# A fused convolution and attention block: the attention's output weight is placed in freed token quarters, later tokens' quarters are split one product later, and the merge takes late tokens first

## The chip, the cores and the metric

The kernel runs on one core of one Trainium2 chip. The metric is the device time of one execution in microseconds (us). The engines are named as the profile names them: PE (TensorE, matrix products), PEld (its weight loads), DVE (VectorE), ACT (ScalarE), POOL (GpSimd) and SP (SyncE, which issues nearly all transfers; its queue is in order, as are those of the others).

## The reference, cut to what matters

One decoder block on x of shape (1, 2048, 1024) in float32. All of its steps, with the names that the kernel uses:

```python
h = rms_norm(x, norm_w) * (1 + scale) + shift            # hT in the kernel
a, b, g_conv, q, k, v, g_attn, m_conv, m_attn = split(h @ w_in)
u = depthwise_causal_conv(a * sigmoid(b), conv_w, conv_b)    # 31 taps
u = silu(layer_norm(u)) * silu(g_conv)
y_conv = u @ w_conv_out                                  # yc
o = dilated_window_attention(rope(rms_norm(q)), rope(rms_norm(k)), v)  # 3 groups x 4 heads
o = sum over groups of softmax(lse) * o                  # the merge
y_attn = (o * silu(g_attn)) @ w_attn_out                 # ya; w_attn_out is 512 x 1024
y = sigmoid(m_conv) * y_conv + sigmoid(m_attn) * y_attn
out = x + gate * (y @ w_out)
```

## The kernel before, in words

Every matrix product is made in three passes: each float32 operand is split into a high part (ACT copies it to the type fp32r) and a low part (DVE or POOL subtracts the high part from the raw value), and high x high, high x low and low x high are added in PSUM. So each operand takes a transfer into a staging tile, a copy on ACT and a subtraction on DVE or POOL before PE can use it.

The kernel goes through these stages:

1. Start: norm and transposition of x into `hT`, high and low, in 16 tiles of 8 KB per partition: `h{hi,lo}{kh}{t}`, with kh the half of the 1024 channels and t the 512-token quarter. They fill the right end of the on-chip memory.
2. Twelve attention units (project, attend) over 16 token blocks each.
3. The merge: 32 steps, each for half the heads (`half` 0 or 1) and one block j of 128 tokens. A step computes the attention's gate (24 matmuls, tile `pzg`, function `z_tokens`, line 367), weighs the three groups (`om`, DVE and ACT), multiplies on POOL (`sg`, L512), transposes on PE (`pta`, L517) and writes `ai_d` to DRAM. The order is all blocks of half 0, then, for half 1, blocks 8 to 15, 4 to 7, 0 to 3. In the last 8 steps the sums S1 to S4 of token quarters (computed earlier, in DRAM as `s_d`) are put over quarters that are no longer read, four pieces of 256 columns each step (`quarter_place`: transfer L831, ACT copy L832, subtraction L833).
4. Two halves of 1024 tokens, each with 20 jobs. A job (`quad`) computes two 128-column blocks of a, b or a gate for 1024 tokens with seven products instead of eight (Strassen-Winograd: the token quarters are A11, A12, A22, S1 to S4; the weight quarters B11 to B22, T1 to T4). A product is 12 matmuls of 512 columns. PSUM copies by ACT (`kept`, L955) and sums on DVE and POOL stand between the products. After product n, `after(n)` prepares product n's weights of the next job (`column_steps`: POOL combines, L913; ACT copies, L918; subtraction L919), and runs some steps of the depthwise convolution on DVE (lines 995 to 1038), which is queued in `conv_todo` when its `ab_quad` is done. In the last job of the first half, `after(n)` instead replaces the quarter just used by the one of the later tokens: four pieces of 512 columns through seven landing tiles (`landing`).
5. Output: `ya` (32 blocks of 12 matmuls, `project`, L1171), layer norm of u beside it, `yc` (32 blocks of 24 matmuls), then the last product with w_out. Before this stage `start_output` closes the convolution's pool `cv`, opens the staging pool `fr` and the weight pool `wap` over its place, and loads and splits `w_attn_out` into `wah`, `wal` (L1098 to L1100). The split high and low parts of `ai_d` are `ai_0` to `ai_3`.

Where tiles of two pools share memory, the later tile waits for the last use of the earlier one. The order on PE is the order in the program (`manual_schedule`); on the other engines a scheduler orders the instructions ahead of time by the times that it expects.

Of the kernel before, what the change touches and what calls it, by code (L numbers as in the profile page):

```python
# [10 lines left out]
F32 = mybir.dt.float32  # L11
# [14 lines left out]
NH = 4  # L26
# [28 lines left out]
def tile_hybrid_block(  # L55
# [61 lines left out]
    with pool("start", side="right") as st:  # L117
# [564 lines left out]

    def quarter_load(half, k, names):
# [14 lines left out]
    for i in range(8):  # L698
        half, k = divmod(i, 4)
        at = NB * 4 + 1 + 12 * i  # L700
        for n, f in ((0, lambda half=half, k=k: quarter_load(half, k, (("21", 0, 0, 1), ("22", 1, 1, 1), ("11", 2, 0, 0)))),
                     (2, lambda half=half, k=k: quarter_sum(half, k, 1, "22", "21", "22", ALU.add)),
                     (4, lambda half=half, k=k: quarter_sum(half, k, 3, "21", "11", "21", ALU.subtract)),
                     (6, lambda half=half, k=k: quarter_sum(half, k, 2, "11", "22", "11", ALU.subtract)),
                     (7, lambda half=half, k=k: quarter_load(half, k, (("12", 1, 1, 0),))),
                     (10, lambda half=half, k=k: quarter_sum(half, k, 4, "12", "12", "11", ALU.subtract))):
            at_step((at + n) // NB, (at + n) % NB, 23, f)
# [118 lines left out]

    def quarter_place(half, name, k, cols, raw, eng):
# [3 lines left out]
        nc.sync.dma_start(raw, quarter_src(half, name, k)[:, cols])  # L831
        nc.scalar.activation(h, raw, AF.Copy)  # L832
        eng.tensor_tensor(l, raw, h.bitcast(F32), op=ALU.subtract)  # L833

    placing = [(n, k, c) for n in ("S2", "S3", "S4", "S1") for k in range(4) for c in (0, 256)]
    for half in range(2):
        for at_j, j in enumerate(orders[half]):
            if half == 0 and j < 3:
                continue
            if half == 1 and at_j >= 8:  # L840
                for i, (n, k, c0) in enumerate(placing[4 * (at_j - 8) : 4 * (at_j - 8) + 4]):
                    raw = wp.tile([P, 384], F32, tag="raw", name=f"raw{n}_{k}_{c0}", bufs=3)[:, :256]
                    quarter_place(0, n, k, slice(c0, c0 + 256), raw, nc.gpsimd if i % 2 else nc.vector)
            hooks = spread_load(loads[j - 4]) if half == 0 and 4 <= j < 4 + KC else {}
            while len(turns) >= 2:
                hooks.setdefault(3, []).append(turns.pop(0))
            pz = merge_z(half, j, cur, hooks)
            if j % 2 == 0:
                state["w"] = weighed.pop((half, j))
                following = pairs[pairs.index((half, j)) + 1 :][:1]  # L850
                coming = [load_pair(*p) for p in following]
            turns += merge_step(half, j, pz, state)
            if j % 2:
                for p, at in zip(following, coming):
                    weighed[p] = merge_weights(*p, at, wk, 2)
            if j == 3 and half == 0:
                queued.__exit__(None, None, None)
                nxt, loads = unit_weights(NG * NH + 1)
        cur = nxt
    for f in turns:  # L860
# [41 lines left out]
    def column_steps(c0, c1):  # L902
# [81 lines left out]
    def conv_parts(half, cb, ut):  # L984
# [16 lines left out]
        def odd(j):  # L1001
            def f():
# [4 lines left out]
                else:  # L1007
                    psum_o = box["o"]
                    if j == HT - 1:
                        box["o"] = cv.tile([P, 512], F32, tag="co", name=f"co{half}_{cb}")  # L1010
                    stt(box["o"], o[:, 2 + j : 514 + j], w, psum_o, op0=ALU.mult, op1=ALU.add)  # L1011
# [78 lines left out]

    big = {}

    def split(h, l, src, eng=nc.vector, raw=None):

# [18 lines left out]

    def big_pairs(tag, n):
        return [[big["wap"].tile([P, D], F32R, tag=f"wb{hl}{k}", name=f"{tag}{hl}{k}") for k in range(n)] for hl in "hl"]

    got, steps = job_columns(0)
    for f in steps:
        f()
    for i, (kind, half, g, cb) in enumerate(jobs):  # L1120
        last_of_half = i + 1 < len(jobs) and jobs[i + 1][1] > half
        nxt, steps = job_columns(i + 1) if i + 1 < len(jobs) else ([], [])
        if i + 1 == len(jobs):
            run_conv(len(conv_todo))
            wraw_c.__exit__(None, None, None)
            start_output()
# [15 lines left out]
        got = nxt  # L1142
    pe_order.__exit__(None, None, None)


    wpool_c.__exit__(None, None, None)
    hpool.__exit__(None, None, None)

# [100 lines left out]
    def load_ai(t, k):  # L1249
        ais[t, k] = parts(t // 2, f"ai{t}_{k}")  # L1250
        raw = gp.tile([P, 512], F32, tag="gt", name="airaw") if t == 0 and k == 3 else None
        split(*ais[t, k], ai_d[k, :, 512 * t : 512 * t + 512], raw=raw)

    wc = [[None] * KC, [None] * KC]

    def load_wc(half, k, h, l):
        split(h, l, w_conv_out[P * k : P * k + P, 512 * half : 512 * half + 512])
        wc[half][k] = h, l
# [42 lines left out]
    def split_wo(half, k):  # L1301
        h, l = (last["wo"][half].tile([P, 512], F32R, name=f"wo{half}{hl}{k}", bufs=1) for hl in "hl")
        split(h, l, w_out[P * k : P * k + P, 512 * half : 512 * half + 512])
        last[half, k] = h, l
# [54 lines left out]
    ys_c.__exit__(None, None, None)  # L1359
    big["pool"].__exit__(None, None, None)  # L1360
    wop_c.__exit__(None, None, None)
    wcp_c.__exit__(None, None, None)


# [26 lines left out]
```

## Time and profile before

| | us |
|---|---|
| median of 3 runs | 2499.51 (2499.28 to 2500.17) |
| the profiled execution's own time | 2502.48 |
| its span, first to last instruction | 2500.7 |
| PE busy | 2400.5 (96%) |
| DVE busy | 1747.3 (70%) |
| ACT busy | 971.0 (39%) |
| POOL busy | 799.2 (32%) |

Busy time is the time in which an engine worked on at least one instruction. A wait row names the instruction that stood still, what released it, the total, the number of waits and the longest. Window rows give the busy time of each engine with the number of its instructions, the clock granted to TensorE (1.00 is full), the share of the 16 DMA engines' time and the rate. The mean granted clock over the span is 0.981.

### The profile page before, as it was taken

To read this page: it belongs to the slowest core of one execution; us is meant where nothing else is said; L and a number is where in the kernel's file an instruction comes from. 1 tells how busy PE (TensorE), PEld (TensorE's weight loads), DVE (VectorE), ACT (ScalarE), POOL (GpSimd) and SP (SyncE) were. 2 spreads that over 40 slices of the span, in tenths; PEclk is the share of its full clock that TensorE was granted. 3 is DMA by queue.
4 is the path that set the end of the run, shared out by engine and by line. 5 is a ranking of instruction groups with operands and counts; after the bars stand their busy time and mean duration, and the time that the engine had idled before them with its cause. 6 is when DMAs were issued, how large, how long until landed. Compare 5 with 4: busy or idle time off the path is not lost.

```text
span 2500.7 us, 39106 instructions
## 1 busy us (share of the span) xinstructions
PE 2400.5 (96%) x12881; PEld 2140.7 (86%) x12881; DVE 1747.3 (70%) x3945; ACT 971.0 (39%) x2738; POOL 799.2 (32%) x925
## 2 busy tenths in 40 slices
PE   6999999999999999999899999799999949999999
PEld 2989999999999999999788888588888828888887
DVE  5855655555556555567699999999999956774333
ACT  4733343344334434445543444544444333331000
POOL 4421111111111111113766766866676400000000
PEclk8999999999999999999999999899999969999999
DMA  7633543454442221136432332623233287867343
GB/s 252 214 114 113 159 125 103 142 153 147 145 129 81 68 64 48 38 106 196 126 97 93 102 102 93 202 85 109 93 95 108 75 275 250 274 201 235 118 145 104
DMA packets 329736, 336.25 MB, mean 134 GB/s; under 512 B 27512, under 2 KB 251032, under 8 KB 329534
## 3 DMA queue, kind: packets, MB, share of 16 engines
q1 hardware_dynamic: 327758, 331.07, 42.3%
q10 hardware_dynamic: 1776, 2.69, 0.3%
q8 instruction: 103, 1.69, 0.3%
q14 instruction: 99, 0.81, 0.1%
HBM read 216.01 MB, written 117.64 MB: 133 GB/s over the span
## 4 chain that ended last, share of the span: by engine, by line
PE 81%; DVE 8%; DMA 5%; ACT 2%; issue 2%; POOL 1%; SPq 0%; DVEq 0%; ACTq 0%; POOLq 0%
PE pz L367 29%; PE out L1171 7%; PE yc L1171 7%; PE paab L949 6%; PE ya L1171 4%; PE pag_g_d L949 3%; PE pcab L949 3%; PE pag_mc_d L949 3%; PE ps L439 3%; PE po L458 3%; PE pag_ma_d L949 2%; PE ptq L429 2%; PE pcg_g_d L949 2%; PE pcg_mc_d L949 1%; PE pbab L949 1%
## 5 line engine op out<-in xcount | busy, mean ns | idle before, releaser
L367 PE MATMUL pz<-wh_u,hT_lo 128*128 128x384 f32 x1536 | 537.1, 350 | 4.9 <-DVE hT_lo L286 2.9
L367 PE MATMUL pz<-wh_u,hT_hi 128*128 128x384 f32 x1536 | 518.3, 337 | 5.6 <-ACT wh_u L343 2.8
L367 PE MATMUL pz<-wl_u,hT_hi 128*128 128x384 f32 x1536 | 519.0, 338 | 0.6 <-DVE wl_u L346 0.6
L395 DVE SCALAR_TENSOR_TENSOR qk<-pz,st,wqk 128x128 f32<-128x128 f32 x384 | 117.0, 346 | 317.9 <-POOL st L111 317.7
L110 POOL TENSOR_SCALAR st<-st 128x2 f32<-128x2 f32 x192 | 48.1, 251 | 812.6 <-ACT sq L384 812.6
L367 PEld LDWEIGHTS pz<-wh_u,hT_hi 128*128 128x128 f32 x1536 | 290.7, 189 | 8.4 <-ACT wh_u L343 3.5
L367 PEld LDWEIGHTS pz<-wh_u,hT_lo 128*128 128x128 f32 x1536 | 289.4, 188 | 8.1 <-DVE hT_lo L286 3.7
L367 PEld LDWEIGHTS pz<-wl_u,hT_hi 128*128 128x128 f32 x1536 | 289.8, 189 | 1.9 <-DVE wl_u L346 1.4
L431 ACT ACTIVATE qkT<-ptq 128x256 f32<-128x256 f32 x192 | 73.9, 385 | 420.3 <-PE ptq L429 419.8
L1027 DVE SCALAR_TENSOR_TENSOR ce<-us,pair_taps,ce 128x512 f32<-128x512 f32 x240 | 179.3, 747 | 2.3
L998 DVE SCALAR_TENSOR_TENSOR ce<-ut,chan,ce 128x512 f32<-128x512 f32 x240 | 178.4, 743 | 0.0
L1011 DVE SCALAR_TENSOR_TENSOR cq<-ut,chan,cq 128x512 f32<-128x512 f32 x208 | 155.7, 748 | 2.7
L384 ACT ACTIVATE sq<-pz 128x128 bf16<-128x128 f32 x384 | 106.2, 276 | 99.1 <-PE pz L367 92.2
L111 POOL TENSOR_TENSOR st<-st,mhalf 128x2 f32<-128x2 f32 x192 | 136.7, 712 | 16.0
L919 POOL TENSOR_TENSOR slT<-wB,shT 128x512 fp32r<-128x512 f32 x80 | 112.1, 1402 | 62.9 <-ACT shT L918 62.6
L913 POOL TENSOR_TENSOR wB<-wB,wB 128x512 f32<-128x512 f32 x80 | 107.7, 1346 | 72.4 <-DVE slB L919 66.6
L918 ACT ACTIVATE shB<-wB 128x512 fp32r<-128x512 f32 x120 | 75.3, 628 | 120.2 <-issue 93.3
L444 ACT ACTIVATE sm<-sm,osb 128x128 f32<-128x128 f32 (+1 forms) x192 | 88.7, 462 | 62.3 <-DVE osb L442 59.7
L1354 DVE TENSOR_TENSOR ot<-out,gate_row 128x512 f32<-128x512 f32 x32 | 22.1, 692 | 116.2 <-PE out L1171 116.2
L458 PE MATMUL po<-lv,pT 128*128 128x128 f32 x600 | 97.2, 273 | 0.0
L918 ACT ACTIVATE shT<-wB 128x512 fp32r<-128x512 f32 x120 | 74.7, 623 | 56.7 <-PE pcab L949 18.3
L458 PEld LDWEIGHTS po<-lv,pT 128*128 128x128 f32 x600 | 93.1, 189 | 0.5 <-issue 0.5
(614 smaller groups left out, 6401.5 us busy)
## 6 DMA issues: line engine op xcount, KB each, us to landing
wB<-in_w_in_dram SPq DMA_DIRECT2D x160, 256.0 KB, 3.4
qkv_d<-qkv SPq DMA_DIRECT2D x128, 192.0 KB, 2.2
raw_u<-in_w_in_dram SPq DMA_DIRECT2D x93, 192.0 KB, 2.9
lqk<-qkv_d SPq DMA_DIRECT2D x128, 128.0 KB, 2.4
acc_d<-osb SPq DMA_DIRECT2D x192, 65.0 KB, 1.7
at<-acc_d SPq DMA_DIRECT2D x64, 195.0 KB, 3.6
wada<-in_w_ada_dram SPq DMA_DIRECT2D x16, 512.0 KB, 8.5
lv<-qkv_d SPq DMA_DIRECT2D x128, 64.0 KB, 1.8
```

The costliest lines, as they stand in the source:

```text
L111: nc.gpsimd.tensor_tensor(dst, scratch[:, :n], mhalf[:, :n], op=ALU.pow)
L367: nc.tensor.matmul(pz[:, :width], part(a, k, P * j, P), w[:, :width], start=(m == 0), stop=(m == 23))
L395: nc.vector.scalar_tensor_tensor(qk[:, 2 * i : 2 * i + 2].rearrange("p a b -> p (a b)"), pz[:, P * i : P * i + P], st[:, 2 + i : 3 + i], w ...
L458: nc.tensor.matmul(po[:, :P], box["pT"][:, P * i : P * i + P], vt, start=(i == 0), stop=(i == nk - 1))
L913: nc.gpsimd.tensor_tensor(dst, x0, x1, op=ALU.subtract)
L918: nc.scalar.activation(h, q[name], AF.Copy)
L919: eng.tensor_tensor(l, q[name], h.bitcast(F32), op=ALU.subtract)
L949: nc.tensor.matmul(ps, w, x, start=(m == 0 and ps.name not in first), stop=(m == 11 and not more), skip_group_check=True)
L998: stt(box["e"], e[:, 1 + j : 513 + j], chan[:, cb, 2 * j : 2 * j + 1], box["e"], op0=ALU.mult, op1=ALU.add)
L1011: stt(box["o"], o[:, 2 + j : 514 + j], w, psum_o, op0=ALU.mult, op1=ALU.add)
L1027: stt(dst, both[:, 1 + j : 513 + j], pair_taps[:, cb, j : j + 1], box["e"], op0=ALU.mult, op1=ALU.subtract if j == 0 else ALU.add)
L1171: nc.tensor.matmul(pz, w, xx, start=(m == 0), stop=(m == len(terms) - 1))
```

## The change

- The tiles of `hT` come from two pools: `hpools[0]` for the quarters t = 0, `hpools[1]` for the others. The first is kept until the end.
- `start_output` and `wap` are gone. The staging pool `fr` is opened before `cv` and has its own place. The split weight of `w_attn_out` lies in the four tiles of `hpools[0]` (`big_pairs`): those of A11 and A12. In the last job, after products 1 to 4, `load_wa` loads and splits one of its four row blocks in two halves, the first subtracted on DVE, the second on POOL. The second half of `w_conv_out` takes the same tiles later (the pool `wap` before).
- In the last job of the first half the pieces' transfers are issued after product n and their splits after product n + 1 (`held`); DVE subtracts three of four, POOL one. The landing tiles are three of pool `gt` and one of `cv` for even n, four scratch tiles for odd n.
- The merge's order is (half 0: 0 to 3), (0: 8 to 15), (1: 8 to 15), (0: 4 to 7), (1: 4 to 7), (1: 0 to 3). The pieces of S1 to S4 are placed in the last 12 steps, three a step in eight of them and two in four; of three, DVE subtracts two and POOL one.
- The weight split of product 3 goes from DVE to POOL.
- Gate jobs after the `ab` jobs of a half: 1, 1, 1, 1, 2, 1, 1, 4 instead of 1, 1, 2, 1, 1, 2, 1, 3.
- The tile `co` of the convolution has one buffer instead of two.

```diff
-    hpool = tc.tile_pool(name="hT", bufs=1, side="right", reuse_waits="tile")
-    hp = hpool.__enter__()
+    hpool_c = [tc.tile_pool(name=f"hT{i}", bufs=1, side="right", reuse_waits="tile") for i in range(2)]
+    hpools = [c.__enter__() for c in hpool_c]
...
-        return hp.tile([P, 4, 512], dtype, tag=f"h{hl}{kh}{t}", name=name)
+        return hpools[t > 0].tile([P, 4, 512], dtype, tag=f"h{hl}{kh}{t}", name=name)
...
-    orders = [list(range(NB)), [*range(8, NB), 4, 5, 6, 7, 0, 1, 2, 3]]
-    pairs = [(half, j) for half in range(2) for j in orders[half][::2]]
+    order = [(half, j) for half, j0, j1 in ((0, 0, 4), (0, 8, NB), (1, 8, NB), (0, 4, 8), (1, 4, 8), (1, 0, 4))
+             for j in range(j0, j1)]
+    pairs = order[::2]
...
-            if half == 1 and at_j >= 8:
-                for i, (n, k, c0) in enumerate(placing[4 * (at_j - 8) : 4 * (at_j - 8) + 4]):
...
-                    quarter_place(0, n, k, slice(c0, c0 + 256), raw, nc.gpsimd if i % 2 else nc.vector)
-            hooks = spread_load(loads[j - 4]) if half == 0 and 4 <= j < 4 + KC else {}
+        if step >= 20:
+            for i, (n, k, c0) in enumerate([placing.pop(0) for _ in range(3 if step < 28 else 2)]):
...
+                quarter_place(0, n, k, slice(c0, c0 + 256), raw, nc.vector if i < 2 else nc.gpsimd)
+        hooks = spread_load(loads[step - 4]) if 4 <= step < 4 + KC else {}
...
+    big = {"fr": ctx.enter_context(pool("fr", bufs=2))}
     cv_c = tc.tile_pool(name="cv", bufs=2, reuse_waits="tile")
...
-        if i % 7 < 4:
-            return scratch(i % 7)
-        return gp.tile([P, 512], F32, tag="gt", name=f"landing{i}")
+        if i % 8 >= 4:
+            return scratch(i % 4)
+        own, tag = (gp, "gt") if i % 8 < 3 else (cv, "ld")
+        return own.tile([P, 512], F32, tag=tag, name=f"landing{i}", bufs=3 if tag == "gt" else 1)
...
-            split(PRODUCTS[n][1], nc.vector if n in (0, 3, 5) else nc.gpsimd)
+            split(PRODUCTS[n][1], nc.vector if n in (0, 5) else nc.gpsimd)
...
-            for _ in range((1, 1, 2, 1, 1, 2, 1, 3)[cb]):
+            for _ in range((1, 1, 1, 1, 2, 1, 1, 4)[cb]):
...
-    def start_output():
-        cv_c.__exit__(None, None, None)
-        big["fr"] = ctx.enter_context(pool("fr", bufs=2))
-        big["pool"] = pool("wap")
-        big["wap"] = big["pool"].__enter__()
-        wh, wl = big_pairs("wa", NH)
-        for k in range(NH):
-            for c0 in (0, 512):
-                sl = slice(c0, c0 + 512)
-                split(wh[k][:, sl], wl[k][:, sl], w_attn_out[P * k : P * k + P, sl])
-        big["wa"] = wh, wl
...
+        rows = {hl: [hpools[0].tile([P, 2, D], F32R, tag=f"h{where}{k}0", name=f"{tag}{hl}{k}") for k in range(n // 2)]
+                for hl, where in (("h", "hi"), ("l", "lo"))}
+        return [[rows[hl][k // 2][:, k % 2] for k in range(n)] for hl in "hl"]
+
+    def load_wa(k):
+        if k == 0:
+            big["wa"] = big_pairs("wa", NH)
+        wh, wl = big["wa"]
+        for c0 in (0, 512):
+            sl = slice(c0, c0 + 512)
+            split_big(wh[k][:, sl], wl[k][:, sl], w_attn_out[P * k : P * k + P, sl], nc.gpsimd if c0 else nc.vector)
...
+            for f in held:
+                f()
+            held.clear()
             if last_of_half:
                 name = PRODUCTS[n][0]
                 for k in range(4):
-                    quarter_place(1, name, k, slice(0, 512), landing(4 * n + k), nc.gpsimd if k % 2 else nc.vector)
+                    args = 1, name, k, slice(0, 512), landing(4 * n + k)
+                    quarter_load(*args)
+                    held.append(lambda args=args, k=k: quarter_split(*args, nc.gpsimd if k == 3 else nc.vector))
             else:
                 run_conv(3 if n < 5 else 4)
+            if i + 1 == len(jobs) and 0 < n <= NH:
+                load_wa(n - 1)
```

`quarter_load` and `quarter_split` are the two parts of `quarter_place`; the earlier functions of the names `quarter_load` and `split` (of the big weights) are now called `quarter_fetch` and `split_big`.

More of the change, by code (lines that the diff above doesn't have):

```diff
@@ L830, in quarter_place @@
         h, l = (x[:, k, cols] for x in quarters[name])
-        nc.sync.dma_start(raw, quarter_src(half, name, k)[:, cols])
         nc.scalar.activation(h, raw, AF.Copy)
         eng.tensor_tensor(l, raw, h.bitcast(F32), op=ALU.subtract)
+    def quarter_place(*args):
+        quarter_load(*args[:5])
+        quarter_split(*args)
     placing = [(n, k, c) for n in ("S2", "S3", "S4", "S1") for k in range(4) for c in (0, 256)]
[L836 to L839, printed above, removed]
-            if half == 1 and at_j >= 8:
-                for i, (n, k, c0) in enumerate(placing[4 * (at_j - 8) : 4 * (at_j - 8) + 4]):
-                    raw = wp.tile([P, 384], F32, tag="raw", name=f"raw{n}_{k}_{c0}", bufs=3)[:, :256]
-                    quarter_place(0, n, k, slice(c0, c0 + 256), raw, nc.gpsimd if i % 2 else nc.vector)
-            hooks = spread_load(loads[j - 4]) if half == 0 and 4 <= j < 4 + KC else {}
[L845 to L859, printed above, removed]
@@ new lines, in tile_hybrid_block @@
+    wts = [cur, None]
+    for step, (half, j) in enumerate(order):
+        if step < 3:
+            continue
+        if step >= 20:
+            for i, (n, k, c0) in enumerate([placing.pop(0) for _ in range(3 if step < 28 else 2)]):
+                raw = wp.tile([P, 384], F32, tag="raw", name=f"raw{n}_{k}_{c0}", bufs=3)[:, :256]
+                quarter_place(0, n, k, slice(c0, c0 + 256), raw, nc.vector if i < 2 else nc.gpsimd)
+        hooks = spread_load(loads[step - 4]) if 4 <= step < 4 + KC else {}
+        while len(turns) >= 2:
+            hooks.setdefault(3, []).append(turns.pop(0))
+        pz = merge_z(half, j, wts[half], hooks)
+        if j % 2 == 0:
+            state["w"] = weighed.pop((half, j))
+            following = pairs[pairs.index((half, j)) + 1 :][:1]
+            coming = [load_pair(*p) for p in following]
+        turns += merge_step(half, j, pz, state)
+        if j % 2:
+            for p, at in zip(following, coming):
+                weighed[p] = merge_weights(*p, at, wk, 2)
+        if step == 3:
+            queued.__exit__(None, None, None)
+            wts[1], loads = unit_weights(NG * NH + 1)
@@ L1251, in load_ai @@
         raw = gp.tile([P, 512], F32, tag="gt", name="airaw") if t == 0 and k == 3 else None
-        split(*ais[t, k], ai_d[k, :, 512 * t : 512 * t + 512], raw=raw)
+        split_big(*ais[t, k], ai_d[k, :, 512 * t : 512 * t + 512], raw=raw)
     wc = [[None] * KC, [None] * KC]
     def load_wc(half, k, h, l):
-        split(h, l, w_conv_out[P * k : P * k + P, 512 * half : 512 * half + 512])
+        split_big(h, l, w_conv_out[P * k : P * k + P, 512 * half : 512 * half + 512])
         wc[half][k] = h, l
@@ L1302, in split_wo @@
         h, l = (last["wo"][half].tile([P, 512], F32R, name=f"wo{half}{hl}{k}", bufs=1) for hl in "hl")
-        split(h, l, w_out[P * k : P * k + P, 512 * half : 512 * half + 512])
+        split_big(h, l, w_out[P * k : P * k + P, 512 * half : 512 * half + 512])
         last[half, k] = h, l
```

25 lines of the change are left out of this document (13 added, 12 removed).

## The prediction

> **What bounds the kernel now.** I read the page's busy digits first. Each digit is a slice of 62.5 us.
>
> ```profile
> span 2500.7 us, 39106 instructions
> ...
> PE   6999999999999999999899999799999949999999
> ...
> DVE  5855655555556555567699999999999956774333
> ...
> PEclk8999999999999999999999999899999969999999
> ```
>
> TensorE (PE) is the bound: 9 nearly everywhere, with dips, counted from 0, at slice 0 (start-up, untouched), 19 (end of the merge), 25 (change of token half) and 32 (the digit 4, from 2000 us on). The last three are the places that the change edits. The list of PE's waits prices them:
>
> ```profile
> PE ya L1171 <- ACT wah L1099: 38.7, 4, 27.9
> PE paab L949 <- ACT spare_hi L955: 11.9, 1, 11.9
> ...
> PE pta L517 <- POOL sg L512: 8.4, 8, 2.4
> ...
> PE pag_ma_d L949 <- ACT spare_lo L955: 4.6, 1, 4.6
> ```
>
> (total, times, longest). 38.7 us are waits for the split output weight of the attention; 11.9 and 4.6 are PSUM copies at the change from first to later tokens; 8.4 lies in the merge. The chain of work and the stage windows show the first of these:
>
> ```profile
> 1996.47 2.73 PE pag_ma_d L949 x12
> ...
> 2007.44 8.99 DMA fraw<-ai_d
> ...
> 2042.82 10.45 PE ya L1171 x33
> ...
> 2054.13 21.81 PE ya L1171 x96
> ```
>
> ```profile
> 1999.20:2042.80 43.60, 4.94 (x9) 2.37 (x9) 20.45 (x30) 15.69 (x25) 0.00 (x0) 0.56 0.90 306
> 1999.20:2135.60 136.40, 97.72 (x418) 78.61 (x419) 83.74 (x133) 46.26 (x74) 2.53 (x4) 0.84 0.79 264
> ```
>
> (Windows: length, busy PE, weight load, DVE, ACT, POOL, PE clock, DMA share, GB/s.) The gate products end at 1999.20; only 9 `ya` matmuls run before 2042.8; from 2054.13 they take 21.81/96 = 0.227 us each.
>
> **Part 1, the output weight.** Before 2053.27 (2042.82 + 10.45) 9 + 33 = 42 matmuls ran, worth 42 x 0.227 = 9.5 us. So this place costs 2053.3 - 1999.2 - 9.5 = 44.6 us, half-speed restart included. The change gives the staging tiles `fr` memory of their own and puts the weight where A11 and A12 of the later tokens lie, which the last gate job reads for the last time in its products 0 and 1. Loads and splits then go after products 1 to 4, in the last 19 us before 1999.2. The engines there:
>
> ```profile
> 1980.10:1999.20 19.10, 19.09 (x85) 15.47 (x83) 18.04 (x26) 5.41 (x9) 1.29 (x1) 1.00 0.17 64
> ```
>
> ```profile
> L1098 SPq DMA_DIRECT2D fraw<-in_w_attn_out_dram x8: 327/330/333, 2019.2 to 2040.0; - x8
> ...
> L1099 ACT ACTIVATE wah<-fraw x8: 629/630/630, 2026.4 to 2043.2; 128x512 fp32r<-128x512 f32 x8
> L1100 DVE TENSOR_TENSOR wal<-fraw,wah x8: 691/693/693, 2027.1 to 2043.8; 128x512 fp32r<-128x512 f32 x8
> ```
>
> ```profile
> wB<-in_w_in_dram SPq DMA_DIRECT2D x160, 256.0 KB, 3.4
> ...
> u_d<-ca SPq DMA_DIRECT2D x16, 512.0 KB, 4.4
> ...
> fraw<-ai_d SPq DMA_DIRECT2D x15, 256.0 KB, 5.8
> ...
> fraw<-in_w_attn_out_dram SPq DMA_DIRECT2D x8, 256.0 KB, 4.7
> ```
>
> ```profile
> L919 POOL TENSOR_TENSOR slT<-wB,shT 128x512 fp32r<-128x512 f32 x80 | 112.1, 1402 | 62.9 <-ACT shT L918 62.6
> ```
>
> Eight copies of 0.63 us (5 us of ACT, which is 5.41 busy of 19.1) and four subtractions of 1.40 on POOL (1.29 busy) are hidden; the four of 0.69 on DVE, 18.04 busy, need the room that part 3 makes. On SP's queue eight issues of 0.33 move ahead of the last `ma_d` stores; if they wait for a staging tile, those stores wait behind them, and through the scratch tiles the PSUM copies (rival E). Two staging tiles feed them, the slower one in rounds of landing + 0.63 + 1.40: 6.7 us with 4.7, 5.4 with the 3.4 that loads of this size take in the jobs. From product 1's end (1999.2 - 5 x 2.72 = 1985.6), the first round fetched ahead (2 x 0.63 + 1.40 = 2.7), the fourth block is ready at 1985.6 + 2.7 + 3 x 5.4 = 2004.5, or 2008.4. PE takes the blocks in turn and needs 2.0 us for the first three, so it waits 2004.5 - 2001.2 = 3 to 7 us; I take 5. What is late next is the attended values `ai` (5.8 + 0.63 + 0.69 = 7.1 us if their transfers start at the end, 0 if before; the chain above already has one of 8.99). The clock: after the 4.6 us wait the chain shows 11 matmuls in 4.79 us.
>
> ```profile
> 1593.53 4.79 PE pag_ma_d L949 x11
> ...
> 1621.40 4.82 PE paab L949 x12
> ...
> 1637.11 2.72 PE pag_g_d L949 x12
> ```
>
> ```profile
> 1218.37 0.50 PE L949 MATMUL paab<-S_hi,slT 128*128 128x512 f32 x1 [1.78 <-POOL slT L919]
> ...
> 1219.64 0.63 PE L949 MATMUL paab<-S_hi,shT 128*128 128x512 f32 x1
> ```
>
> At full speed 11 are 2.5 us, so a restart costs 2.3 (4.79) or 2.1 (4.82 against 2.72). Cost left 5 + 2.3 = 7.3; gain 37.3 (bounds 44.6 - 2 and 44.6 - 16). The Trainium skill (TensorE: Matmul & The Clock Gate, "What's actually happening") lets the clock fall only after about 3.4 us idle; the trace has slow matmuls (0.63 us) behind a wait of 1.78 us. By that rule a gap under 3.4 us costs no restart and the gain is 2.3 us larger; I go by the rows.
>
> Given back: from 1999.2 to 2042.8 DMA moved 306 GB/s x 43.6 us = 13.3 MB ahead of need, and now `ya` starts without that lead. All that stage moved 264 x 136.4 = 36.0 MB; 8 weight transfers (2.1 MB) go out of it and 0.5 MB of convolution, 33.4 MB remain. At 264/0.79 = 334 GB/s that takes 100 us, against 87 (32 blocks x 2.72) + 7.3 = 94 us of PE. Not all is due by the end (norm values for the next stage), so stalls of 0 to 20 us; I take 5. The fastest stretch:
>
> ```profile
> 2010.00:2020.00 10.00, 0.00 (x0) 0.00 (x0) 2.05 (x3) 1.89 (x3) 0.00 (x0) 0.50 1.05 399
> ```
>
> At 399 it is 84 us, and nothing stalls. The Trainium skill (DMA: Bandwidth & Descriptors, "Where 436 GB/s comes from") sets 358 GB/s as the limit between HBM and SBUF. This row exceeds it; by 358 an estimate is 93 us, also no stall, and the sum would be 5 us better.
>
> Part 1 sums to 37.3 - 5 = 32.
>
> **Part 2, the later tokens' quarters.** 28 pieces (256 KB) are loaded and split within the last gate job. ACT's wait rows and the window:
>
> ```profile
> 1580.00:1621.40 41.40, 24.90 (x100) 19.74 (x98) 36.92 (x45) 25.24 (x45) 37.14 (x26) 0.80 0.78 237
> ```
>
> ```profile
> ACT A_hi L832 <- DMA spare_hi<-h_d: 6.4, 3, 3.3
> ACT A_hi L832 <- DMA landing<-h_d: 4.3, 2, 2.6
> ```
>
> ```profile
> L833 POOL TENSOR_TENSOR S_lo<-spare_hi,S_hi 128x512 fp32r<-128x512 f32 x5 | 7.7, 1549 | 0.0
> ...
> L833 DVE TENSOR_TENSOR S_lo<-spare_hi,S_hi 128x512 fp32r<-128x512 f32 x5 | 6.2, 1237 | 2.0 <-ACT S_hi L832 2.0
> ```
>
> Cost now: 41.4 - 24.9 = 16.5 idle, plus 2.3 and 2.1 of slow clock = 20.9 us. Mechanism: ACT's queue is in order; a split's copy waits for its transfer (longest 3.3 us) and the copy of PSUM that PE needs (L955) stands behind. Splitting one product (2.72 us) later covers all but 0.6 of the longest wait, and A22's splits come behind the next job's first PSUM copy. What stays: 28 pieces and 8 weight loads are 9.4 MB, in 19.05 us 495 GB/s: at 399 they take 23.6, 4.6 us too long, at 334 28 us, 9 too long, less what the eight landing places fetch ahead. DVE now gets 21 subtractions instead of 14: 21 x 1.24 = 26 us against 19, POOL 7 x 1.55 = 11 instead of 22. Left: 2 to 15 us; I take 7. Gain 14. Job order: four gate jobs instead of three follow the last convolution block, so the convolution has drained here; a lag on DVE inside the half reaches PE only through two-deep buffers, cost 0 while it stays under one block (38 us).
>
> **Part 3, a weight split (n = 3) from DVE to POOL in all 40 jobs.**
>
> ```profile
> L919 DVE TENSOR_TENSOR slT<-wB,shT 128x512 fp32r<-128x512 f32 x40 | 54.9, 1372 | 14.7 <-ACT shT L918 8.6 <-POOL wB L913 5.9
> ```
>
> ```profile
> 1625.00:1999.20 374.20, 374.19 (x1649) 309.12 (x1647) 361.45 (x515) 153.58 (x272) 237.60 (x182) 1.00 0.29 94
> ```
>
> DVE is 97% busy there (361/374) and loses 40 x 1.37 = 55 us; POOL, 237.6 of 374 us (12.1 us per job of 19.05), gains 1.40 per job: 13.5. PE never waited in this window (374.19 busy), so the price is 0, hidden by weights made one job ahead; if POOL's order spoils that, up to 1.4 per job. DVE's room is what lets the convolution's tail and part 1's subtractions end by 1999.2; I count that in the 5 us of waiting there. One buffer for `co` instead of two: written and read by DVE only, 0.
>
> **Part 4, the merge.** Late tokens first frees places 8 steps earlier: 32 pieces go over 12 steps (3, then 2) instead of 8 (4 each).
>
> ```profile
> 1160.00:1204.20 44.20, 39.05 (x310) 38.24 (x309) 33.97 (x109) 25.31 (x80) 18.58 (x25) 0.96 0.63 192
> ```
>
> ```profile
> L833 POOL TENSOR_TENSOR S_lo<-rawS,S_hi 128x256 fp32r<-128x256 f32 x13 | 10.1, 777 | 12.9 <-ACT S_hi L832 8.3 <-DVE S_lo L833 2.4 <-DVE om L507 2.1
> ...
> L833 DVE TENSOR_TENSOR S_lo<-rawS,S_hi 128x256 fp32r<-128x256 f32 x14 | 8.2, 586 | 3.4 <-ACT S_hi L832 3.4
> ```
>
> ```profile
> raw_ga<-in_w_in_dram SPq DMA_DIRECT2D x16, 128.0 KB, 2.7
> ```
>
> Cost now 44.2 - 39.05 = 5.2, and 4% of clock, 1.8: 7. POOL, which makes `sg` for the transposes, loses 8 of 16 pieces (6.2 us); DVE, 77% busy, gains 8 x 0.59 = 4.7 us over four more steps. I take 3 gained; bounds +7 and -4, because half 1's last weight slice is used one step after its load instead of five (2.7 us of transfer and some 1.2 of split). The handover after 1204.2 stays: its weights still wait for the last step's.
>
> **Sum.** 32 + 14 + 0 + 3 = 49 us. The profiled execution took 2502.5 us, 3.0 over the median 2499.5; 2502.5 - 49 = 2453.5, on the median 2450.
>
> **Rivals.** A: the output stage becomes bound by transfers. For: 0.90 DMA share before PE even starts, and 33.4 MB at 334 GB/s exceed PE's time. Against: 399 GB/s was reached. If the lead (13.3 - 2.6 = 10.7 MB, 32 us at 334) is only half hidden, 20 us come back instead of 5: 2465. B: the wait for the weight becomes one for `ai`, whose tiles lie where convolution and weight buffers end: another 15 us idle in part 1, also 2465. C: the half change still stalls, since 495 GB/s and DVE's 26 us can't fit in 19: part 2 gives 3, not 14: 2461. D, slower: POOL in conv jobs. Its in-order queue waits for ACT (62.6 us) and DVE; if the added split makes each of 40 jobs longer than 19.05 by x, the whole gain is gone at x = 49/40 = 1.2 us, that is POOL at 20.3 us per job while its work is 13.5. At the full 1.4: 2506. E: the splits in the last job block ACT's PSUM copies, so that PE waits there what it waited after: part 1 gives 5, 2477.
>
> **Chances.** Forecast 0.56 (own range 2436 to 2459); A 0.13, B 0.06, C 0.10, D 0.07 (0.03 of it with x near 1.2, no change), E 0.03, better than 2436 0.05. All but D and E end at least 30 us ahead; a measurement here tells 0.2% (5 us) from no change. Faster 0.93, same 0.03, slower 0.04. The range 2434 to 2476 leaves out D, E, the worst of A and B together, and the best tail.
>
> **What would show it.** Right: the wait of `ya` on `wah` under 10 us, the slice that holds this place at 8 or 9, `ya` starting within 8 us of the last gate product; `paab <- spare_hi` under 6; `pta <- sg` near 5; no new PE wait on `slT` between jobs. Wrong: `ya` or the norm's matmuls (`pc`) waiting for DMA or DVE later in the stage (A), `ya` on `ai` (B), L955 still behind L832 (C), PE waiting on POOL through the jobs (D), PE idle before the last gate product (E).

## The result, and the profile after

The changed kernel takes 2458.96 us (median of 4 runs, 2455.92 to 2460.94) against 2499.4 us of the kernel before on the same chip (2497.68 to 2500.17): a ratio of 0.9838, 95% interval 0.9821 to 0.9855, 40 us less. The forecast was 2450, with a range of 2434 to 2476. The profiled execution of the changed kernel took 2458.03 us (span 2455.9).

The page's busy digits, the rows that stood first in the prediction:

```profile
span 2455.9 us, 39171 instructions
...
PE   6999999999999999999899999999999999999999
...
DVE  5855655555556555557599999999999967874333
...
PEclk8999999999999999999999999999999999999999
```

The digit 4 at slice 32 is gone, and so is the dip of the change of halves (slice 25). The list of PE's waits (total, times, longest):

```profile
PE pta L517 <- POOL sg L512: 11.2, 8, 2.5
...
PE paab L958 <- ACT spare_hi L964: 3.4, 1, 3.4
PE pag_ma_d L958 <- ACT spare_lo L964: 2.8, 1, 2.8
...
PE ya L1185 <- ACT ai_0h L1106: 2.4, 1, 2.4
```

38.7 us of waits for `wah` have become 2.4 us for `ai_0h`; 11.9 and 4.6 at the change of halves have become 3.4 and 2.8; the merge's 8.4 is 11.2. The chain of work over the start of the output stage (start, length, what):

```profile
1974.17 3.05 DMA fraw<-in_w_attn_out_dram
1977.24 0.64 ACT wah L1106
1977.95 1.31 POOL wal L1107
1979.27 2.79 DMA fraw<-in_w_attn_out_dram
...
1990.58 12.97 PE ya L1185 x41
2003.55 0.86 PE pm L1207 x2
2004.41 22.47 PE ya L1185 x96
...
2181.34 92.78 PE yc L1185 x396
```

The weight runs through the two staging tiles in rounds of transfer, copy and subtraction while the last gate products still run, as the prediction wrote it. The last gate product ends at 1987.4. Up to the norm's first product `pm` at 2003.5 are 16.1 us, of which 42 `ya` products (one ahead of the row x41) need 9.5 at 0.227: the place costs 6.6 us (forecast 7.3, before 44.6). The whole stage, and the change of halves in equal windows of the changed kernel (length, busy PE, PEld, DVE, ACT, POOL, PE clock, DMA share, GB/s):

```profile
1987.40:2089.00 101.60, 98.99 (x423) 78.69 (x423) 72.75 (x117) 41.87 (x68) 4.72 (x5) 0.97 0.95 331
1570.00:1630.00 60.00, 53.83 (x218) 43.51 (x217) 53.87 (x62) 36.01 (x65) 47.63 (x33) 0.91 0.66 203
```

and the second window of the kernel before:

```profile
1570.00:1630.00 60.00, 43.50 (x174) 35.00 (x173) 54.06 (x63) 32.91 (x59) 48.80 (x35) 0.83 0.69 206
```

PE works 10.3 us more in these 60 us. Between the two traces the span falls by 44.8 us (2500.7 to 2455.9). By milestones: up to the merge +1.9 (the same code); merge and handover to the first `paab` product +0.8; from there to the last gate product -14.5 (790.4 to 775.9); from there to `pm` -38.0 (54.1 to 16.1); the rest of `ya` +2.3; `yc` and `out` +2.7. The two last signs were not expected in this form. By medians the gain is 40 us; the profiled execution of the kernel before lay 3.0 us above its median, that of the changed kernel 0.9 below its own, so the sums over traces come out larger.

### The profile page after: what moved, and what is told of

The parts are those of the page before. It is cut to its first block, busy times and chain, and to the rows that moved or that the text cites. A ratio compares the mean times of both kernels' runs of the same rounds, so it can differ in the third digit from the quotient of the medians.

```text
span 2455.9 us, 39171 instructions
## 1 busy us (share of the span) xinstructions
PE 2401.1 (98%) x12881; PEld 2140.9 (87%) x12881; DVE 1702.4 (69%) x3916; ACT 970.0 (39%) x2738; POOL 833.3 (34%) x954
## 4 chain that ended last, share of the span: by engine, by line
PE 89%; DMA 3%; ACT 2%; DVE 1%; POOL 1%; issue 1%; SPq 0%; DVEq 0%; POOLq 0%; ACTq 0%
PE pz L367 30%; PE yc L1185 7%; PE out L1185 7%; PE paab L958 7%; PE ya L1185 4%; PE pcab L958 4%; PE pag_mc_d L958 4%; PE pag_g_d L958 4%; PE pag_ma_d L958 3%; PE ps L439 3%; PE po L458 3%; PE pcg_g_d L958 2%; PE pcg_mc_d L958 2%; PE ptq L429 2%; PE pzg L367 2%; PE pbab L958 2%
## 5 line engine op out<-in xcount | busy, mean ns | idle before, releaser
L928 POOL TENSOR_TENSOR slT<-wB,shT 128x512 fp32r<-128x512 f32 x120 | 163.1, 1367 | 55.8 <-ACT shT L927 55.8
```

Of the source, the lines that this page charges most:

```text
L928: eng.tensor_tensor(l, q[name], h.bitcast(F32), op=ALU.subtract)
```

## The experiments

Each run names the part that it undoes or does alone. Ratios are to the kernel before on the same chip, with 95% intervals; differences in us come from medians. The runs stand on three chips, on which the kernel before takes 2499.0, 2501.0 and 2499.7 us, so two runs are compared by their gains over the kernel before.

**The changed kernel again**, as the yardstick, without an edit.

> The changed kernel once more, as the yardstick for the runs beside it: 2459 us, 2456 to 2461, and a ratio of 0.984 to the kernel before. Its trace should again show `ya` and `yc` products at a mean of 234 ns from start to start, no wait of a `ya` product for a weight, and two short waits at the change of halves.

2458.3 us, ratio 0.9838 (0.9824 to 0.9851), 40.7 us less than the kernel before, as in the first comparison. Its trace has no wait of `ya` for a weight and two waits of 3.4 us at the change of halves, as expected.

**Part 1 alone**, on the kernel before:

```diff
-    hpool = tc.tile_pool(name="hT", bufs=1, side="right", reuse_waits="tile")
+    hpool_c = [tc.tile_pool(name=f"hT{i}", bufs=1, side="right", reuse_waits="tile") for i in range(2)]
...
-            wraw_c.__exit__(None, None, None)
-            start_output()
...
+            if i + 1 == len(jobs) and 0 < n <= NH:
+                load_wa(n - 1)
```

> The kernel before with part 1 alone: the output weight goes into the freed quarters during the last job, on alternate VectorE and GpSimd. The merge, the splits of the quarters at the change of halves and the engine of the n = 3 weight split are as before. Theory: the place between the last gate product and the first product of the stage is worth 37.9 us by the two traces, and the slower products of `ya` and `yc` take 5 of them back, so -33 us, 2463 to 2468; the half change still shows its 21 us of loss (waits of 6.6 and 8.0 us). Rival: the gain needs the room that part 3 makes on VectorE (97% busy in the jobs before); without it the convolution's tail and the weight's subtractions come late, the place keeps a wait of 15 to 20 us, and the time is 2475 to 2485.

The edit also gives `co` its one buffer. 2491.8 us, ratio 0.9971 (0.9960 to 0.9983): 7 us faster, not 33. The theory failed; the rival, which named the room on DVE, was nearer and still hoped for too much. Its PE waits:

```profile
PE ya L1171 <- ACT ai_0h L1098: 23.4, 1, 23.4
PE paab L950 <- ACT spare_hi L956: 11.6, 2, 11.5
```

The wait for the weight has become a wait for `ai`: rival B of the prediction, with 23 us where it was priced at 15. Its chain shows what stands ahead of `ai`, and two rows that come back below:

```profile
2001.31 4.79 DMA ma_d<-gt
2006.17 8.04 DMA ma<-ma_d
2014.23 7.88 DMA fraw<-ai_d
...
2035.97 22.49 PE ya L1171 x96
...
2213.29 92.78 PE yc L1171 x396
```

**The changed kernel without part 3** (the n = 3 weight split back on VectorE):

```diff
-            split(PRODUCTS[n][1], nc.vector if n in (0, 5) else nc.gpsimd)
+            split(PRODUCTS[n][1], nc.vector if n in (0, 3, 5) else nc.gpsimd)
```

> The changed kernel with the n = 3 weight split back on VectorE. The forecast costed its move to GpSimd at nothing for the jobs. Theory: in the jobs no matmul waits either way, but VectorE comes to the change of halves and to the last job with its convolution taps late, so the half change loses 2 to 6 us more (subtraction of the quarters late) and the first weight of the output stage up to 3 more: 2461 to 2467. Rival: VectorE at 97% is still enough, and the time is the same within 2 us of 2459.

2483.5 us, ratio 0.9927 (0.9915 to 0.9940), 17.5 us less than the kernel before: 23 us of the 41 are gone with one number of the code, far outside both expectations. The wait is that of part 1 alone:

```profile
PE ya L1185 <- ACT ai_0h L1106: 23.0, 1, 23.0
```

The order of time on DVE and on SP of this run, around the convolution's last output `ca`:

```profile
1999.16 0.75 DVE L1036 SCALAR_TENSOR_TENSOR ca<-us,pair_taps,ce 128x512 f32<-128x512 f32 x1
1999.94 1.22 DVE L1047 TENSOR_TENSOR usum<-usum,ca 128x1024 f32<-128x1024 f32 x1
```

```profile
1993.36 2.89 SPq L1201 DMA_DIRECT2D d<-u_d  x5
1997.65 0.33 SPq L1293 DMA_DIRECT2D ma<-ma_d  x1
1998.03 1.53 SPq L1201 DMA_DIRECT2D d<-u_d  x3
2000.60 2.98 SPq L1238 DMA_DIRECT2D gg<-g_d  x3
2004.66 0.32 SPq L1043 DMA_DIRECT2D u_d<-ca  x1
2005.30 10.59 SPq L1105 DMA_DIRECT2D fraw<-ai_d  x5
```

and the same of the changed kernel:

```profile
1982.11 1.23 DVE L1047 TENSOR_TENSOR usum<-usum,ca 128x1024 f32<-128x1024 f32 x1
```

```profile
1982.10 0.33 SPq L1043 DMA_DIRECT2D u_d<-ca  x1
1984.52 0.33 SPq L1105 DMA_DIRECT2D fraw<-in_w_attn_out_dram  x1
1984.90 0.42 SPq L1105 DMA_DIRECT2D fraw<-ai_d  x1
```

With n = 3 on DVE the convolution ends at 2001.2, ten us after the last gate product (1990.8), instead of 1983.3, four us ahead of it (1987.4). In both, the loads of `ai` into `fraw` are issued behind the store of its last output. But SP's order differs too: without part 3 thirteen further loads (two of `ma`, eight of `d`, three of `gg`) and the store of `ca` stand between the last weight load and the first three `ai` loads into `fraw`; in the changed kernel these come right behind the weight, with only a gate store in between. So the wait reaches PE through SP's queue, not through a subtraction of the weight. And it is the order of that queue, with the transfers ahead in it, that holds `ai`, not a wait for DVE: from 1988 us to the `ai` load at 2005.30 the waits of SP are for the last gate values (3.3 us) and for transfers (5.7 us, half of them the row below), none is for DVE, and `ca`, written by 1999.91, had stood ready for 4.7 us when its store went out.

```profile
SPq L1238 <- DMA d<-u_d: 2.9, 3, 1.0
```

In part 1 alone it is the same: `ca` is written by 2006.26, its store goes out at 2010.89, and from 1998 to 2014.4 no wait of SP is for DVE. The order is fixed ahead of time, and the one number of the code changed it. That the scheduler put the loads so because it expected DVE late is likely but not shown, and what DVE's lateness would cost under the order of the changed kernel wasn't tried. This run also shows PE waits inside the jobs that the forecast put at nought (a `pag_g_d` wait of 2.9 us for `spare_lo`); from the first `paab` product to the last gate product it takes 783.1 us against 775.9.

**Part 3 alone**, and **parts 1 and 3**, both on the kernel before; the first has only this edit, the second this and the edit of part 1:

```diff
-            split(PRODUCTS[n][1], nc.vector if n in (0, 3, 5) else nc.gpsimd)
+            split(PRODUCTS[n][1], nc.vector if n in (0, 5) else nc.gpsimd)
```

> The kernel before with part 3 alone: the n = 3 weight split on GpSimd in all 40 jobs, nothing else. The forecast put its own price at 0, so by it 2499. Theory now: VectorE runs behind in the jobs, and how far behind it is when the last gate product ends sets when the convolution's buffers come free; in the kernel before, the output weight and the attended values land over these buffers. With 55 us of work less VectorE ends its convolution some 18 us earlier, and the wait of `ya` for `wah` shrinks by about as much: 2479 to 2487. At the change of halves nothing changes (wait of 10 to 12 us stays). Rival: alone it moves nothing, because the weight's own loads and splits take as long wherever they begin: 2496 to 2502.

> The kernel before with parts 1 and 3: the output weight in the freed quarters during the last job, and the n = 3 weight split on GpSimd. The merge, the quarters' splits and the order of jobs are as before. Theory: the two need each other. Part 1 alone gave 7 us, and the run of the changed kernel without part 3 lost 25, with a wait of 23 us of `ya` for `ai_0h` in both. Together that wait is under 6 us and the time 2463 to 2469; what then lacks to 2458 is the half change, whose wait of `paab` for `spare_hi` stays at 8 to 12 us. Rival: the parts add up without depending on each other: 2491.8 less what part 3 gives alone in the run beside this one.

2480.3 us, ratio 0.9917 (0.9903 to 0.9930), and 2468.8 us, ratio 0.9871 (0.9858 to 0.9885), both times within the theory's bounds; the waits at the change of halves, 13.6 and 13.9 us, lie a little above what was expected. Part 3, which the forecast priced at 0, is worth 19 us by itself, and part 1 then adds 12. "The two need each other" was too strong: 0.9971 x 0.9917 = 0.9888, with an uncertainty of its own, lies just outside the measured interval, so most of the gain adds up. The place itself, from the last gate product to `pm`, shows it best. Windows of part 1 alone, part 3 alone, both, and the changed kernel without part 3:

```profile
1999.40:2035.10 35.70, 12.27 (x44) 9.46 (x44) 15.18 (x22) 7.17 (x13) 1.26 (x1) 0.67 0.83 287
```

```profile
1991.80:2027.50 35.70, 14.90 (x43) 9.93 (x44) 13.47 (x21) 11.99 (x20) 0.00 (x0) 0.62 0.97 337
```

```profile
1994.40:2011.20 16.80, 12.80 (x44) 9.33 (x44) 4.50 (x7) 4.71 (x9) 1.26 (x1) 0.80 1.00 337
```

```profile
1990.80:2026.00 35.20, 11.84 (x44) 9.20 (x44) 16.72 (x24) 7.26 (x13) 1.26 (x1) 0.66 0.84 287
```

The first number is the length. Less 42 x 0.227 = 9.5 us of work, the place costs 44.6 before, 26.2 with part 1, 26.2 with part 3, 7.3 with both: each takes off 18 to 19 us of a sequence. The sequence is read so: first what DVE has left over and the queue behind it, then the weight's rounds; part 3 shortens the one (the convolution ends at 1986.4 with part 3 alone, 2008.1 before), part 1 takes the other out. With part 3 alone, `ya` still waits for the weight:

```profile
PE ya L1171 <- ACT wah L1099: 14.6, 2, 12.5
PE paab L949 <- ACT spare_hi L955: 13.6, 1, 13.6
```

**The quarters' splits right behind their loads again**, on the changed kernel:

```diff
-                    quarter_load(*args)
-                    held.append(lambda args=args, k=k: quarter_split(*args, nc.gpsimd if k == 3 else nc.vector))
+                    quarter_place(*args, nc.gpsimd if k == 3 else nc.vector)
```

> The changed kernel with the quarters' splits issued right behind their loads again, as before, all else as changed (three of four subtractions on VectorE, seven landing tiles plus one). Theory: with ScalarE in order, the copies of the next weights' first rounds stand behind copies that wait for a landing, so the half change loses its 21 us again instead of 11: +10 us, 2469 (2465 to 2473), with a wait of about 7 us of a matmul for ScalarE at line 963 or thereabouts. Rival: the landing tiles and the subtractions set the pace, and holding a split back only moves the wait; then within 2 us of 2459.

2458.4 us, ratio 0.9834 (0.9821 to 0.9847): no difference. The theory, the forecast's own mechanism for part 2, is wrong, at least beside the other edits there, and the rival right. PE is 52.64 us busy in the window of 60:

```profile
1570.00:1630.00 60.00, 52.64 (x217) 42.67 (x216) 53.64 (x59) 35.88 (x66) 45.64 (x32) 0.94 0.68 205
```

**The subtractions there on alternate engines again**, on the changed kernel:

```diff
-                    held.append(lambda args=args, k=k: quarter_split(*args, nc.gpsimd if k == 3 else nc.vector))
+                    held.append(lambda args=args, k=k: quarter_split(*args, nc.gpsimd if k % 2 else nc.vector))
```

> The changed kernel with the quarters' subtractions at the change of halves on alternate engines again (two of four on GpSimd in place of one). Theory: the second short wait there (3.4 us at the first paab product of half 1) goes back to a landing whose subtraction on VectorE came late; with two of four on GpSimd VectorE has four subtractions fewer, and the place loses 2 to 4 us less: 2455 to 2457. Rival: GpSimd, which also splits five of seven weights of the next job there, becomes the late one (some 2 us for each subtraction of 512 columns), and the loss grows by 3 to 6: 2462 to 2465.

2461.0 us, ratio 0.9844 (0.9831 to 0.9858), 40.0 us less than the kernel before against 40.7 of the yardstick: the times show no difference. The trace of one execution does show a loss in this place, and for the rival. Its window and its chain at the first product of half 1:

```profile
1570.00:1630.00 60.00, 48.28 (x193) 38.58 (x193) 40.20 (x48) 34.23 (x63) 52.26 (x37) 0.89 0.63 193
```

```profile
1602.33 3.41 POOL S_lo L837 x2
...
1610.43 1.25 POOL S_lo L837
1611.69 5.43 DMA landing<-h_d
1617.15 0.63 ACT A_hi L836
```

POOL is late with the subtractions, so a landing tile comes free late, its transfer starts late, and ACT stands before that transfer's copy with the copy of PSUM behind it; PE waits 7.8 us for `spare_hi` instead of 3.4. DVE has the room (40 of 60 us busy). PE's busy time goes 43.5 (before), 48.3 (this), 53.8 (changed): by these windows moving one subtraction in four from POOL to DVE is half of the gain at this place, though the times above don't confirm it. With parts 1 and 3 alone this wait was 13.9, with part 1 alone 11.5, so neither of them helps here. The other half is not explained: it lies with what no run here took back by itself, such as the order and number of the landing tiles.

**The old job order**, on the changed kernel:

```diff
-            for _ in range((1, 1, 1, 1, 2, 1, 1, 4)[cb]):
+            for _ in range((1, 1, 2, 1, 1, 2, 1, 3)[cb]):
```

> The changed kernel with the old number of gate jobs behind each paab job (1, 1, 2, 1, 1, 2, 1, 3 in place of 1, 1, 1, 1, 2, 1, 1, 4). Theory: the order of the jobs decides only how many gate jobs lie between the last paab job of a half and the end, in which the convolution's tail runs out. With three instead of four there are 19 us less of room for it: VectorE then still runs taps in the last job and the weight's subtractions are 2 to 8 us late, 2461 to 2467. Rival (the forecast, which put this at nought): within 2 us of 2459.

2458.2 us, ratio 0.9827 (0.9814 to 0.9841): no difference, as the forecast had it. `ya`'s wait for `ai_0h` is 5.6 instead of 2.4 us, too little to show in the time.

**The merge's old order**, on the changed kernel, with the old four pieces a step on alternate engines:

```diff
-    order = [(half, j) for half, j0, j1 in ((0, 0, 4), (0, 8, NB), (1, 8, NB), (0, 4, 8), (1, 4, 8), (1, 0, 4))
-             for j in range(j0, j1)]
+    order = [(half, j) for half, j0, j1 in ((0, 0, NB), (1, 8, NB), (1, 4, 8), (1, 0, 4)) for j in range(j0, j1)]
...
-        if step >= 20:
+        if step >= 24:
```

> The changed kernel with the merge's old order of token blocks, its old four pieces per step in the last eight steps, and the subtractions on alternate engines. The forecast had the new order gaining 3 us: by it 2462. The two traces, milestone by milestone, show the merge and the handover to the first job together at +0.8 us, so by them 2458, 2456 to 2460. Its trace tells how the parts of that nought stand: if the old order shows fewer waits of `pta` for `sg` (8.4 us before, 11.2 after) but a granted clock under 1 at the first job again, gain and loss cancel; if the waits stay at 11, they belong to another part of the change.

2457.1 us, ratio 0.9835 (0.9822 to 0.9848): no difference. Its waits of `pta` for `sg` come to 9.8 us, against 10.2 in the changed kernel beside it: the order of the merge moves neither the time nor this wait by an amount that these runs can tell.

**The place of a weight in memory**, on the changed kernel: the pool `wcp` (convolution output's weight for columns 0 to 511) on the left side, at lower addresses:

```diff
-    wcp_c, wcp = right("wcp")
     lnp_c, lnp = right("lnp")
+    wcp_c = pool("wcp")
+    wcp = wcp_c.__enter__()
```

> The changed kernel with the pool of the convolution output's weight for the first 512 output columns opened on the left side of the on-chip memory rather than the right; the tiles opened behind it on the left move up by its size. Nothing is computed differently. Theory: the products' pace (234 ns against 227 from start to start) goes by where the weights lie, not by load on the transfers or on VectorE; then `yc` of the first 512 columns goes from 234 to 227 ns, 384 products by 7.6 ns, -2.9 us: 2456, with `yc` of the other columns and `ya` still at 234. Rival: the pace comes from what runs beside the products (transfers at 331 GB/s, VectorE's evictions); then all of `yc` stays at 234 ns and the time stays within 1.5 us of 2459.

2456.2 us, ratio 0.9821 (0.9807 to 0.9836); the time doesn't resolve 2.9 us, the trace does. The last 396 `yc` products, half of them with this weight:

```profile
2177.00 91.35 PE yc L1186 x396
```

and the kernel before:

```profile
2227.55 91.28 PE yc L1171 x396
```

With 92.78 us in the changed kernel that is 0.2307 us for each product instead of 0.2343, so 0.227 for the half that moved. The theory holds: the pace went with the place of the weight, while the share of the transfers (0.65) and DVE's work (49.4 us) are the same in both stretches of 396 products.

**Two versions meant to beat both kernels.** The first has the edit above and takes two of the eight weight transfers through tiles of the pool `gt`:

```diff
+            raw = gp.tile([P, 512], F32, tag="gt", name=f"wraw{k}") if 2 * k + c0 // 512 in (2, 5) else None
-            split_big(wh[k][:, sl], wl[k][:, sl], w_attn_out[P * k : P * k + P, sl], nc.gpsimd if c0 else nc.vector)
+            split_big(wh[k][:, sl], wl[k][:, sl], w_attn_out[P * k : P * k + P, sl], nc.gpsimd if c0 else nc.vector, raw)
```

> The changed kernel with two edits meant to be faster: the convolution output's weight for the first 512 columns on the left side (as in the run before, 2.8 us in `yc`), and two of the eight transfers of the attention's output weight staged in tiles of the pool `gt` instead of the ring of two `fraw` tiles. Theory: the start of `ya` is paced by that ring (four rounds of landing, copy and subtraction); with four places rather than two the weights are split 4 us earlier, the `ai` loads behind them are issued earlier, and `ya` no longer waits at its start: the place costs 2 to 3 us rather than 7, and the time is 2450 to 2453. Rival: the last gate stores, not the ring, hold the `ai` loads (they stand between them in SP's order); then only the pace changes: 2455 to 2457.

The second also has `nc.vector if n == 0` in the weight split.

> The kernel of the run before this one, and the n = 5 weight split on GpSimd too, so that VectorE keeps only n = 0. Theory: at the change of halves VectorE is still the late one (21 subtractions beside its convolution taps); another 1 us per job off it (some 30 us in all) lets it come there with less behind it, so the second wait there goes, -3 to -4 us: 2447 to 2450. Rival: GpSimd gets 14.8 us of work per job of 19 and with six of seven weight splits becomes the late one at the change of halves: 0 to +5 us against the run before, 2451 to 2457.

2454.2 us, ratio 0.9817 (0.9803 to 0.9830), and 2454.1 us, ratio 0.9812 (0.9799 to 0.9826): both 45.6 us less than the kernel before, some 5 us better than the yardstick's 40.7, with intervals that overlap its own; the pace of `yc` accounts for 2.8 of them. Neither theory came true. The ring of staging tiles was not the limit: in the first one the place still costs 7.5 us (17.0 less 9.5). The first one's chain:

```profile
1985.13 0.32 SPq L1082
...
1985.50 3.89 DMA fraw<-ai_d
...
1990.10 12.76 PE ya L1187 x42
```

The weight is off the chain, and the `ai` load waits behind the gate store of line 1082 in SP's queue, as its rival said. In the second VectorE ends the convolution at 1970, 13 us earlier, and the time doesn't change.

## Why the prediction was right in sum, and where its steps failed

The sum, 49 us, was 40 by medians. Four of its terms are wrong in size or cause and partly cancel, so that part of the agreement is luck.

- **Part 3, priced at 0: the step that failed.** "The price is 0, hidden by weights made one job ahead" looked only for a loss on POOL. POOL didn't become late in the jobs (rival D), as forecast. But the row quoted there, DVE 361 of 374 us busy, had a second reading: DVE had work left at the end of the stage (before, the convolution ends at 2008.1, 9 us after the last gate product). The move is worth 19 us alone, 24 with part 1 and 23 with all the rest, each by gains over the kernel before on its chip. In single traces that is 18 to 19 at the start of the output stage and 4 to 7 in the jobs (from the first `paab` product to the last gate product 790.4 us before, 791.0 with part 1 alone, 786.4 with part 3 alone, 786.1 with both). At the start of the stage it works through the order of SP's queue, as the run without part 3 shows. The text named this room as a condition ("need the room that part 3 makes") and put it into "the 5 us of waiting"; it is half of the 37.3 claimed for part 1.
- **Part 1, 37.3 at its place: right for the pair, 18.4 for itself.** What is left, 6.6 us against 7.3, agrees in sum and not in its parts: the weight was ready 2.2 us after the last gate product (at 1989.6), where 5.3 was worked out, and no product waited for it; PE waited 2.4 us for `ai` instead, and the slow clock behind it cost more than the 2.3 put down. Rival B was listed at 0.06 as a separate case; it is just what happens to part 1 where DVE is late (23.4 and 23.0 us).
- **Given back, 5 us by stalls on transfers: right size, wrong cause, so luck.** The `ya` stage moved 331 GB/s at a DMA share of 0.95, near the 334 forecast, and PE waited for none of it. The 358 GB/s that the Trainium skill gives (DMA: Bandwidth & Descriptors, "Where 436 GB/s comes from") was not reached over the whole stage, though 10 us of the kernel before exceeded it (399); it speaks for the no-stall side, which was the right one. What was given back is pace: 96 `ya` products in 22.47 us instead of 21.81 (2.6 us for 384), and 1.50 us for 396 `yc` products (2.9 for 768).
- **Part 2, 14: measured 10, by another mechanism.** Holding the splits back changes nothing. The engine of the subtractions is half of it by the windows; the cause of the other half is open. Rival C (only 3 gained, since DVE has 26 us of work for 19) did not come true either: with as many subtractions on DVE the wait fell.
- **Part 4, 3: measured 0.** The waits of `pta` rose instead of falling to 5; the old order on the changed kernel shows that the order isn't the cause of gain or loss. The job order at 0 stands, with part 3 in place. One buffer for `co` is in every run with part 1 and was not tried by itself.
- **The clock.** The place after has a mean PE clock of 0.79 in the trace (16.1 us from 1987.4), and the 41 products of the chain take 12.97 us, 3.4 more than at 0.234 each, behind a wait of 2.4 us. The Trainium skill's rule (TensorE: Matmul & The Clock Gate, "What's actually happening"), a fall only after some 3.4 us idle, would have given no restart here; the forecast's 2.3 us from the rows was nearer.

So by the traces: -38.0 (parts 1 and 3 together), -10.3 (part 2), -4.2 (rest of the jobs, as part 3 alone gives), +5.0 (pace), +2.7 (merge, and what lies ahead of it) make -44.8 of span.

## What to carry to other kernels

An engine that is 97% busy in a stage can carry work past the stage's end without holding up TensorE in it. Here one subtraction per job taken off it was worth 19 to 24 us, most of it at the start of the next stage, whose loads were then queued in another order. When a wait is removed, follow the in-order transfer queue and ask what stands ahead of the next operand in it, and whether the queue waits for the late engine or only for the order that it was given. Two parts that shorten one sequence should be priced on that sequence together, and each tried alone. And holding an instruction back gained nothing here, where the tile that it waits for is freed by another engine.

## What the runs showed of the hardware that was not expected

The pace of matrix products depended on where the weights lay in on-chip memory. Products of one shape ran at 0.227 us in `ya` before (21.81/96) and at 0.234 as soon as the weight lay in the quarters' place: with part 1 alone (22.49/96, DVE and merge as before), and in the changed kernel (22.47/96). With part 3 alone, the weight in its old place, they ran at the old pace:

```profile
2028.32 21.81 PE ya L1171 x96
```

Moving the convolution output's weight for columns 0 to 511 the other way took its products from 0.234 to 0.227; in the kernel before it was the other columns' weight that lay low (in `wap`) and ran at 0.227, and this one at 0.234. The two stretches of 396 products above have the same transfers and the same work on DVE. Which property of the place matters is open: by the compiled programs the slow places lay at the upper end of each partition's memory, but in the `out` stage, which takes 177.5 us for 768 products (0.231 on the mean) in all of these kernels, some operands lower down were slow too, and in the jobs, whose weights lie lower on that side, 12 products take 2.72 us (0.227). No single address bound fits, and no run here changed one address and nothing else.
